# Eight-row and one-row matmuls widened to 128 rows, and two reorderings of VectorE's queue, in a Fourier and attention encoder

## The chip, the core and the metric

The kernel runs on one core of a Trainium2 chip. The metric is the device time of one execution, in microseconds (us), lower is better. Five engines run their own instruction queues side by side: TensorE (PE in the profile, its weight loads are PEld), VectorE (DVE), ScalarE (ACT), GpSimd (POOL) and SyncE (SP, which here only issues DMAs).

## What is computed

The reference runs two independent sequences of 512 tokens with 1024 features through two layers. Layer 0 mixes tokens by a 2-D Fourier transform, layer 1 by attention with 8 query heads and 2 key heads; each is followed by an MLP with a squared ReLU and 4096 hidden features:

```python
def fourier_mix(h, w_out):
    hg = h.reshape(B, S, 8, 128)                       # 8 groups of 128 features
    f = jnp.fft.fft2(hg, axes=(1, 3), norm="ortho").real
    return f.reshape(B, S, 1024) @ w_out

def sq_relu_mlp(h, w_up, w_down):
    a = jnp.maximum(h @ w_up, 0)
    return (a * a) @ w_down

x = x + fourier_mix(rms_norm(x), w_out);  x = x + sq_relu_mlp(rms_norm(x), ...)   # layer 0
x = x + gqa_attention(rms_norm(x), ...);  x = x + sq_relu_mlp(rms_norm(x), ...)   # layer 1
return rms_norm(x)
```

All arithmetic is float32. The kernel gets its precision out of float32r operands: each operand is split into a high and a low part, and a product is three matmuls (high by high, high by low, low by high). `split` (L80 to L82) does this: ScalarE casts the high part (L81), then VectorE, or in some places GpSimd, subtracts it from the source for the low part (L82).

## The kernel before, in words

**Shared tiles.** On-chip tiles come from pools with a fixed number of buffers: 38 of one size for activations and operands (`slot`), 8 half-size ones (`tm`), 5 for raw weights (`raw`), 4 for split weights (`w`), 8 PSUM banks (`ps`). A load waits until a buffer of its pool is free. The compiler's scheduler fixes each engine's order from the program's order and its own estimates; inside `tc.manual_schedule(engines=...)` the named engines keep the written order of the instructions of that block.

**The Fourier stage** (L273 to L690, all five engines in written order). The transform over the 512 tokens uses the symmetry of cosine and sine: `Front` normalizes the input, folds feature d with its mirror image and token s with token 512 - s, and leaves an even part `ee`, an odd part `oo` (two chunks c of 128 tokens each) and eight columns `ny`. `transform(q)` (L440) then works for sequence q:

- `seq_nyq` and `seq_part` (L399, L403) multiply by the cosine and sine tables: for each of four blocks j of 128 features, and each chunk c, three matmuls into `o` and three into `v`. With c = 1, `seq_even` adds the token in the middle, whose cosine is +1 or -1: two matmuls over one single row (L395, L396), row 0 of `oo` (or `ny`) against row 0 of the table `altT`.
- `seq_evac` (L411) splits `o` and `v` out of PSUM into operands `a` and `b`.
- `feat_stage` (L419) transforms over the features in a group: three matmuls on `a`, two over eight rows (L423, L424: `nyqT`, 8 rows, against `an`, the split of `seq_nyq`'s eight rows), three on `b`, two into `en` (L427, L428). Its results are split into `uv[q, j]`. `nyq_out` (L434) makes `un[q]` of `en`.
- `even_outs` and `odd_outs` (L535, L538) multiply `uv` by the output weights, which `Fold` has folded meanwhile: sums and differences of weight rows on GpSimd and VectorE (L479, L482), high parts on ScalarE (L486), low parts on VectorE (L490) or GpSimd (L82). `even_outs` needs `uv[q, 3]` for its last block k = 3, and at the end `un[q]` (L532).

For sequence 0 the results wait aside (`Aside.move`) and are added to the residual later: the even half on GpSimd (`ev.add`, L571 to L573), the odd half on VectorE (`od.add`, L568 and L569). `ev.add` runs during `transform(1)`, and `od.add(j)` stands in VectorE's queue inside `transform(1)`, ahead of the splits of `feat_stage(j)` (`between`, L454 to L464). Then follow `even_outs(1, ...)`, whose results VectorE adds (L543, L544), `odd_outs(1, ...)` (L548, L549), the sums of squares, and the normalized operands of the MLP (`Blocks`).

**The MLP** multiplies pairs of 128-row blocks in a 2-by-2 scheme with seven block products in place of eight: sums of operand blocks on the one side, sums of weight blocks on the other. `first_product` (L751) does 14 pairs p. `Pair.rest(p)` (L815) has five products, each 12 matmuls of 128x512: `ob`, `oc`, `od`, then `a22` on top of `oc`, then `s4` on top of `od`. After each product VectorE adds the result up: u2 (L819), u3 (L821), u3 again (L829), v (L838), t (L843). The fourth product needs L821 to have read `oc`, the fifth needs L829 to have read `od`. Between these stand the weight sums and splits of the next pair: `sums_23` (L796 to L798), `split_23`, `sum_4` (L802), `split_1`, `split_4` (all L82). For p < AHEAD = 6 VectorE keeps the written order; from p = 6 on, each pair has seven products in `rest`'s period and the scheduler orders VectorE. `Pair.out` then makes sums of the results on GpSimd (L851 to L854) and writes seven spill tensors, on ScalarE's and SP's queues.

The last pair, 13, has no next pair. After it, four `Regular` blocks r0 to r3 (L859) go through `w_up` without the scheme, and `second_product` begins, which reads the spilled operands back: `moving` (L948) loads an operand by DMA and splits it. The generator `ahead` (L1032) issues the first of these loads early; the operands of its first groups are b11, b21 (four pairs) and t2, t1, t3, b22, t4 (two pairs).

Of the kernel before, what the change touches and what calls it, by code (L numbers as in the profile page):

```python
# [18 lines left out]
P = 128  # L19
# [20 lines left out]
def trunk_kernel(ctx, tc, x_in, xt_in, y_out, dcos, dsin, feat, rope, gfour, gcol, grow, gfin,  # L40
# [19 lines left out]
    def slot(shape, dt):  # L60
        return act.tile(shape, dt, tag="u4", name=nm("u"))
# [235 lines left out]
    gr, rcos, rsin, rft, gc = begin()  # L297
    tabs = [slot([P, D], F32R) for _ in range(2)]
    cosT = [t[:, :516].rearrange("p (a b) -> p a b", a=2) for t in tabs]
    altT = tabs[0][0:1, 516:774]  # L300
    pickT = tabs[1][:, 516:594]
    sinT = slot([P, 2, 512], F32R)
    fslot = slot([P, D], F32R)
    ft = fslot[:, :512].rearrange("p (a b) -> p a b", a=2)
    nyqT = fslot[0:8, 512:1024]

    def table_cos():
        for c in range(2):
            split(cosT[c][:, 0], cosT[c][:, 1], rcos[:, c * 258 : (c + 1) * 258])
        nc.scalar.copy(altT, rcos[0:1, 516:774])  # L310

    def table_sin():
        split(sinT[:, 0], sinT[:, 1], rsin)

    def table_feat():
        split(ft[:, 0], ft[:, 1], rft[:, :256])
        nc.scalar.copy(nyqT, rft[0:8, 334:846])
        nc.scalar.copy(pickT, rft[:, 256:334])


# [77 lines left out]

    def seq_nyq(q, c, o):  # L399
        seq_even(o[0:8, :258], [ny[q, c][:, i, 0:8] for i in range(2)],  # L400
                 [ny[q, 0][0:1, i, 8:16] for i in range(2)], c)

    def seq_part(q, j, c, o, v):  # L403
        js = slice(j * P, (j + 1) * P)
        seq_even(o[:, :258], [ee[q, c][:, i, js] for i in range(2)],
                 [oo[q, 0][0:1, i, js] for i in range(2)], c)
        cs = slice(c * 256, (c + 1) * 256)
        mm3(v[:, :256], oo[q, c][:, 0, js], oo[q, c][:, 1, js],
            sinT[:, 0, cs], sinT[:, 1, cs], c == 0, c == 1)
# [9 lines left out]
    def feat_stage(q, j, a, b, an, en):  # L419
        u, v = ps(), ps()  # L420
        mm3(u[:, :258], ft[:, 0, 0:P], ft[:, 1, 0:P], a[:, 0], a[:, 1], True, False)
        nyt = nyqT[:, j * P : (j + 1) * P]
        nc.tensor.matmul(u[:, :258], nyt, an[0:8, 0], start=False, stop=False)  # L423
        nc.tensor.matmul(u[:, :258], nyt, an[0:8, 1], start=False, stop=True)  # L424
        mm3(v[:, :256], ft[:, 0, P:], ft[:, 1, P:], b[:, 0], b[:, 1], True, True)
        ent = pickT[:, 6 - 2 * j : 78 - 2 * j]
        nc.tensor.matmul(en[0:72, :258], ent, a[:, 0], start=j == 0, stop=False)  # L427
        nc.tensor.matmul(en[0:72, :258], ent, a[:, 1], start=False, stop=j == 3)  # L428
        t = slot([P, 2, 512], F32R)
        split(t[:, 0, 0:257], t[:, 1, 0:257], u[:, :257])  # L430
        split(t[:, 0, 257:], t[:, 1, 257:], v[:, 1:256])
        uv[q, j] = t

    def nyq_out(q, en):  # L434
# [2 lines left out]
        nc.vector.tensor_sub(t[64:72], en[64:72, :258], f32(t[64:72]))  # L437
        un[q] = t

    def transform(q, mid=lambda: None, between=lambda j: None):  # L440
        on, ov = ps(), [(ps(), ps()) for _ in range(3)]
        seq_nyq(q, 0, on)
        for j in range(3):
            seq_part(q, j, 0, *ov[j])
        mid()
        en = ps()
        seq_nyq(q, 1, on)
        an = slot([P, 2, 258], F32R)
        split(an[0:8, 0], an[0:8, 1], on[0:8, :258])
        ab = []  # L450
        for j in range(3):
            seq_part(q, j, 1, *ov[j])
            ab.append(seq_evac(*ov[j]))
        between(0)  # L454
        feat_stage(q, 0, *ab[0], an, en)
        o3 = ps(), ps()
        for c in range(2):
            seq_part(q, 3, c, *o3)
        between(1)
        feat_stage(q, 1, *ab[1], an, en)  # L460
        ab.append(seq_evac(*o3))
        between(2)
        feat_stage(q, 2, *ab[2], an, en)
        between(3)  # L464
        feat_stage(q, 3, *ab[3], an, en)
        nyq_out(q, en)
# [275 lines left out]
    def product(o, w, h, first=True):  # L742

        n = len(h)
        for k in range(n):
            sl = slice(k * P, (k + 1) * P)
            for i, (x, y) in enumerate(((0, 0), (0, 1), (1, 0))):
                nc.tensor.matmul(o, w[x][:, sl], h[k][y], start=first and k + i == 0,  # L748
                                 stop=k == n - 1 and i == 2, skip_group_check=not first)

    def first_product(l, blocks, rows, ahead):  # L751
        def b(name):
            return [(h[0][:, i], h[1][:, i]) for h in blocks.b[name] for i in range(2)]
# [10 lines left out]
        class Pair:  # L764
# [47 lines left out]
                self.s4 = h[:, 0], h[:, 1]  # L812
                split(*self.s4, self.x4)

            def rest(self, nxt):  # L815
                ob, oc, od = ps(), ps(), ps()
                u2, u3, t = tm(), tm(), self.t
                product(ob, self.s2, b("t2"))
                nc.vector.tensor_add(u2, ob, t[:, 0])  # L819
                product(oc, self.s3, b("t3"))  # L820
                nc.vector.tensor_add(u3, oc, u2)  # L821
                if self.p >= AHEAD:
                    self.second()
                if nxt:
                    nxt.sums_23()
                product(od, self.s1, b("t1"))
                if nxt and nxt.p >= AHEAD:
                    nxt.split_row()
                nc.vector.tensor_add(u3, od, u3)  # L829
                if nxt:  # L830
                    nxt.split_23()
                squares(u3, u3)
                product(oc, self.a22, b("t4"), False)
                if nxt:
                    nxt.sum_4()
                    nxt.split_1()
                v = tm()
                nc.vector.tensor_add(v, oc, u2)  # L838
                squares(v, v)
                if nxt:  # L840
                    nxt.split_4()
                product(od, self.s4, b("b22"), False)
                nc.vector.tensor_add(t[:, 0], od, u2)  # L843
                squares(t[:, 0], t[:, 0])
                return t[:, 1], t[:, 0], v, u3
# [72 lines left out]
        for p, pair in enumerate(pairs[:-1]):  # L918
# [9 lines left out]
                last[0].load()  # L928
            pair.out(*done)

        pairs[-1].first()
        with tc.manual_schedule(engines={ET.DVE}):
            done = pairs[-1].rest(None)
        with tc.manual_schedule(engines={ET.SP}):
            for r in last[1:]:
                next(ahead)
                r.load()
            for _ in ahead:
                pass
            pairs[-1].out(*done)  # L940
# [3 lines left out]
    def second_product(l, blocks, rows):  # L944
# [84 lines left out]
            for op in (("b11", "b21"), ("t2", "t1", "t3", "b22", "t4"))[i][slice(*ops)]:  # L1029
                b[op] = moving(op, g, n)  # L1030

        def ahead():  # L1032
            n = SUM_GROUPS[0][1]
            group(0, 0, ROW_GROUPS[0][1])
            yield
            group(1, 0, n, (0, 2))
            yield
            group(1, 0, n, (2, 5))
            yield
            early[0, 0, 0] = row_raw(0, 0, ROW_GROUPS[0][1])  # L1040
            for q in range(NSEQ):
                residual(q, 0)
            early[1, 0, 0] = sums_raw(0, 0, n)
            for q in range(NSEQ):
                residual(q, 1)

        first_product(l, blocks, rows, ahead())
        e += [tm() for _ in range(4)]
        for _, i, m, g, n in sorted(steps):
            if m == 0 and g > 0:  # L1050
# [498 lines left out]
```

## Time and profile before

| | us |
|---|---|
| three runs, median (lowest to highest) | 1784.64 (1781.79 to 1785.09) |
| the profiled execution | 1783.47 |
| its span, first to last instruction | 1781.7 |
| around the span (difference) | 1.77 |
| TensorE busy, share of the span | 1722.3, 97% |
| VectorE busy | 1225.2, 69% |
| mean granted TensorE clock | 0.982 |

The span is what the profile shows; the 1.77 us around it are taken to be unchanged. The profile's times are us from the start of the span. In a timeline a row has start, duration, engine, line, operation, output<-inputs, shape and count, and in brackets the engine's idle time before it and what ended it. In a table of windows, each row has the window, its length, and for each engine its busy time and (in brackets) the instructions begun, then the granted clock of TensorE as a share of full speed. In the table of waits a row has who waited for whom: total us, times, longest.

### The profile page before, as it was taken

Reading aid. Unit: us, or ns where it says so; the run is one execution under the profiler, and the core shown is the slowest. Engines: PE = TensorE matmul, PEld = TensorE weight load, DVE = VectorE, ACT = ScalarE, POOL = GpSimd, SP = SyncE. Lnnn points to the kernel's source line nnn. Section 1 sums busy time; section 2 is a strip of 40 time slices with the busy share of each in tenths; the row PEclk is TensorE's granted clock in tenths of the full one; section 3 lists DMA queues with packets and bytes.
Section 4 is the critical chain, followed back from the end, with each engine's and each line's share of the span. In section 5 each row is a group of like instructions: output and inputs, shape, how many; then the busy total and the mean of one; then the engine's idle time right before and its main releaser. Section 6 shows DMA issues by size and latency. Waiting matters only on the chain. (4 is left out here: it accounts for less than half of the span.)

```text
span 1781.7 us, 22113 instructions
## 1 busy us (share of the span) xinstructions
PE 1722.3 (97%) x7918; PEld 1417.7 (80%) x7918; DVE 1225.2 (69%) x1777; ACT 867.0 (49%) x1531; POOL 478.4 (27%) x382
## 2 busy tenths in 40 slices
PE   5999999999999999999999999999999999999997
PEld 4887877887778778878877888787788877878777
DVE  6867777455787686666578853687845478686765
ACT  4556545445534242345687733564544554343234
POOL 3550143223221111243334302204332232111103
PEclk7889999999999999999999999999999999999999
DMA  7234355337865353431100122224544486364232
GB/s 279 102 119 136 113 184 198 144 136 265 286 199 195 130 183 101 166 124 48 48 24 1 49 94 107 95 95 180 204 154 148 182 320 230 128 224 163 99 107 95
DMA packets 101670, 260.83 MB, mean 146 GB/s; under 512 B 10024, under 2 KB 10024, under 8 KB 101560
## 3 DMA queue, kind: packets, MB, share of 16 engines
q1 hardware_dynamic: 87160, 233.20, 37.4%
q10 hardware_dynamic: 14400, 26.22, 3.9%
q8 instruction: 62, 1.02, 0.2%
q14 instruction: 48, 0.39, 0.1%
HBM read 187.03 MB, written 72.35 MB: 146 GB/s over the span
## 5 line engine op out<-in xcount | busy, mean ns | idle before, releaser
L748 PE MATMUL ps<-u,w 128*128 128x512 f32 x4752 | 1094.6, 391 | 14.6 <-DVE u L960 8.0
L748 PEld LDWEIGHTS ps<-u,w 128*128 128x128 f32 x4752 | 889.0, 188 | 213.3 <-issue 9.3
L81 ACT CAST w<-raw 128x1024 fp32r<-128x1024 f32 (+2 forms) x250 | 232.0, 932 | 488.5 <-PE ps L748 299.4
L82 DVE TENSOR_TENSOR w<-raw,w 128x1024 fp32r<-128x1024 f32 (+2 forms) x246 | 274.1, 1117 | 65.7 <-ACT w L81 64.9
L82 DVE TENSOR_TENSOR u<-u,u 128x1024 fp32r<-128x1024 f32 x122 | 162.3, 1346 | 25.4 <-ACT u L81 25.2
L960 DVE TENSOR_TENSOR u<-ps,u 128x512 f32<-128x512 f32 x160 | 109.7, 687 | 97.8 <-PE ps L748 97.2
L81 ACT CAST u<-u 128x1024 fp32r<-128x1024 f32 x123 | 126.5, 1050 | 81.6 <-DMA u<-spill_b 61.9
L851 POOL TENSOR_TENSOR u<-u 128x512 f32<-128x512 f32 x28 | 38.3, 1367 | 446.2 <-ACT u L762 446.2
L1005 POOL TENSOR_TENSOR raw<-raw,raw 128x512 f32<-128x512 f32 (+1 forms) x32 | 43.4, 1356 | 419.0 <-DVE raw L1004 376.2
L76 PE MATMUL ps<-u,u 128*128 128x512 f32 (+2 forms) x392 | 153.2, 393 | 2.4 <-ACT u L561 1.6
L77 PE MATMUL ps<-u,u 128*128 128x512 f32 (+2 forms) x392 | 147.2, 376 | 1.5 <-DVE u L82 1.5
L78 PE MATMUL ps<-u,u 128*128 128x512 f32 (+2 forms) x392 | 147.2, 375 | 0.6 <-POOL u L82 0.6
L154 POOL TENSOR_TENSOR t<-t,t 128x512 f32<-128x512 f32 (+1 forms) x56 | 75.8, 1354 | 213.6 <-ACT t L152 153.8
L82 DVE TENSOR_TENSOR u<-ps,u 128x512 fp32r<-128x512 f32 (+4 forms) x126 | 76.6, 627 | 23.9 <-ACT u L81 22.8
L76 PE MATMUL ps<-u,w 128*128 128x512 f32 (+2 forms) x256 | 91.4, 357 | 0.9 <-ACT w L81 0.9
L732 DVE TENSOR_TENSOR u<-ps,u 128x512 f32<-128x512 f32 (+1 forms) x64 | 41.9, 656 | 72.7 <-PE ps L78 72.7
L78 PE MATMUL ps<-u,w 128*128 128x512 f32 (+2 forms) x256 | 90.8, 356 | 0.5 <-DVE w L82 0.5
L77 PE MATMUL ps<-u,w 128*128 128x512 f32 (+2 forms) x256 | 90.8, 355 | 0.0
L76 PEld LDWEIGHTS ps<-u,u 128*128 128x128 f32 x392 | 78.7, 201 | 15.1 <-ACT u L81 2.5
L77 PEld LDWEIGHTS ps<-u,u 128*128 128x128 f32 x392 | 79.1, 202 | 13.1 <-DVE u L82 4.2
L748 PE MATMUL ps<-u,u 128*128 128x512 f32 x336 | 82.0, 393 | 7.6 <-DVE t L829 7.6
L78 PEld LDWEIGHTS ps<-u,u 128*128 128x128 f32 x392 | 78.6, 201 | 12.8 <-POOL u L82 0.8
(210 smaller groups left out, 2141.9 us busy)
## 6 DMA issues: line engine op xcount, KB each, us to landing
raw<-w_up SPq DMA_DIRECT2D x84, 512.0 KB, 4.0
u<-spill_t SPq DMA_DIRECT2D x56, 512.0 KB, 6.6
raw<-w_sum SPq DMA_DIRECT2D x48, 512.0 KB, 3.6
spill_t<-u SPq DMA_DIRECT2D x84, 256.0 KB, 2.0
u<-spill_b SPq DMA_DIRECT2D x42, 512.0 KB, 5.8
spill_b<-t ACTq DMA_DIRECT2D x56, 256.0 KB, 2.0
park<-u SPq DMA_DIRECT2D x24, 512.0 KB, 2.6
raw<-w_row SPq DMA_DIRECT2D x24, 512.0 KB, 3.4
```

The lines of the kernel that those rows point to most:

```text
L76: nc.tensor.matmul(out, lh, rh, start=first, stop=False)
L77: nc.tensor.matmul(out, lh, rl, start=False, stop=False)
L78: nc.tensor.matmul(out, ll, rh, start=False, stop=last)
L81: nc.scalar.copy(dst_hi, src)
L82: eng.tensor_sub(dst_lo, src, f32(dst_hi))
L154: nc.gpsimd.tensor_add(acc[q][:, :n], acc[q][:, :n], s[:, :n])
L732: nc.vector.tensor_add(x[:, :n], o[:, :n], x[:, :n])
L748: nc.tensor.matmul(o, w[x][:, sl], h[k][y], start=first and k + i == 0, stop=k == n - 1 and i == 2, skip_group_check=not first)
L851: nc.gpsimd.tensor_sub(t[:, 0], b12, b11)
L960: nc.vector.tensor_add(x, o, x)
L1005: nc.gpsimd.tensor_sub(a11, a11, a21)
```

## The change

It has three parts.

1. **128 rows.** `altT` and `nyqT` become tables with all 128 partitions (the rows beyond the first one, or the first eight, are zero in the input tables), and the matmuls at L395, L396, L423 and L424 take all 128 rows of `oo`, `ny` and `an`. `an` is allocated once ahead of both transforms, and GpSimd sets it to zero at the start of the kernel.
2. **`rest` of every pair but the last.** `sums_23` of the next pair moves ahead of the product `oc` and its sum L821 (for p = 0 it stays behind L821), and `split_23` moves from behind L829 to ahead of the product `od`, so ahead of L829; `split_row` (p >= 5) comes behind it.
3. **The last pair.** VectorE and SP keep the written order there, and `ahead` is stepped from inside `rest`: b11's load and split and r1's load ahead of the product `od` and L829; b21's and r2's load ahead of L838; t2's, t1's and r3's load ahead of the last product and L843. The rest of `ahead` follows after it.

```diff
-    altT = tabs[0][0:1, 516:774]
+    altT = tabs[0][:, 516:774]
-    nyqT = fslot[0:8, 512:1024]
+    nyqT = fslot[:, 512:1024]
...
-        nc.scalar.copy(altT, rcos[0:1, 516:774])
+        nc.scalar.copy(altT, rcos[:, 516:774])
-        nc.scalar.copy(nyqT, rft[0:8, 334:846])
+        nc.scalar.copy(nyqT, rft[:, 334:846])
...
-                 [ny[q, 0][0:1, i, 8:16] for i in range(2)], c)
+                 [ny[q, 0][:, i, 8:16] for i in range(2)], c)
-                 [oo[q, 0][0:1, i, js] for i in range(2)], c)
+                 [oo[q, 0][:, i, js] for i in range(2)], c)
...
-        nc.tensor.matmul(u[:, :258], nyt, an[0:8, 0], start=False, stop=False)
-        nc.tensor.matmul(u[:, :258], nyt, an[0:8, 1], start=False, stop=True)
+        nc.tensor.matmul(u[:, :258], nyt, an[:, 0], start=False, stop=False)
+        nc.tensor.matmul(u[:, :258], nyt, an[:, 1], start=False, stop=True)
...
+    an = slot([P, 2, 258], F32R)
+    nc.gpsimd.memset(f32(an), 0.0)
     def transform(q, mid=lambda: None, between=lambda j: None):
-        an = slot([P, 2, 258], F32R)
...
-            def rest(self, nxt):
+            def rest(self, nxt, fill=iter(())):
                 product(ob, self.s2, b("t2"))
                 nc.vector.tensor_add(u2, ob, t[:, 0])
+                if nxt and self.p > 0:
+                    nxt.sums_23()
                 product(oc, self.s3, b("t3"))
                 nc.vector.tensor_add(u3, oc, u2)
                 if self.p >= AHEAD:
                     self.second()
                 if nxt:
-                    nxt.sums_23()
-                product(od, self.s1, b("t1"))
+                    if self.p == 0:
+                        nxt.sums_23()
+                    nxt.split_23()
                 if nxt and nxt.p >= AHEAD:
                     nxt.split_row()
+                next(fill, None)
+                product(od, self.s1, b("t1"))
                 nc.vector.tensor_add(u3, od, u3)
-                if nxt:
-                    nxt.split_23()
                 squares(u3, u3)
                 product(oc, self.a22, b("t4"), False)
                 if nxt:
                     nxt.sum_4()
                     nxt.split_1()
+                next(fill, None)
                 v = tm()
                 nc.vector.tensor_add(v, oc, u2)
                 squares(v, v)
+                next(fill, None)
                 if nxt:
                     nxt.split_4()
                 product(od, self.s4, b("b22"), False)
...
+        ahead = ahead(last[1:])
         pairs[-1].first()
-        with tc.manual_schedule(engines={ET.DVE}):
-            done = pairs[-1].rest(None)
+        with tc.manual_schedule(engines={ET.DVE, ET.SP}):
+            done = pairs[-1].rest(None, ahead)
         with tc.manual_schedule(engines={ET.SP}):
-            for r in last[1:]:
-                next(ahead)
-                r.load()
             for _ in ahead:
                 pass
...
-        def ahead():
+        def ahead(regular):
             n = SUM_GROUPS[0][1]
-            group(0, 0, ROW_GROUPS[0][1])
+            group(0, 0, ROW_GROUPS[0][1], (0, 1))
+            regular[0].load()
+            yield
+            group(0, 0, ROW_GROUPS[0][1], (1, 2))
+            regular[1].load()
             yield
             group(1, 0, n, (0, 2))
+            regular[2].load()
             yield
             group(1, 0, n, (2, 5))
-            yield
             early[0, 0, 0] = row_raw(0, 0, ROW_GROUPS[0][1])
```

More of the change, by code (lines that the diff above doesn't have):

```diff
@@ L1045, in ahead @@
                 residual(q, 1)
-        first_product(l, blocks, rows, ahead())
+        first_product(l, blocks, rows, ahead)
         e += [tm() for _ in range(4)]
```

## The prediction

> **What bounds the kernel now.** First the page, then the waits of TensorE.
>
> ```profile
> span 1781.7 us, 22113 instructions
> ...
> PEclk7889999999999999999999999999999999999999
> ```
> ```profile
> PE ps L748 <- DVE t L829: 7.6, 10, 1.7
> ```
>
> TensorE is the busiest engine throughout, so time can come only from its clock or its waits. Two entries touch the change: the clock of the first three slices (45 us each), and 7.6 us of waits for L829 in ten places. Next, four windows of the Fourier stage (two from transform(0), two round transform(1)), and single matmuls.
>
> ```profile
> 28.86:32.27 3.41, 3.41 (x13) 2.50 (x12) 1.53 (x4) 1.30 (x4) 3.41 (x2) 0.50 0.88 348
> 49.34:52.75 3.41, 3.41 (x17) 3.41 (x17) 3.28 (x7) 0.72 (x3) 3.41 (x2) 0.50 0.01 2
> 76.65:80.06 3.41, 1.83 (x14) 1.22 (x13) 2.84 (x7) 2.40 (x6) 0.00 (x0) 1.00 0.07 26
> 100.54:103.95 3.41, 3.41 (x17) 3.21 (x16) 1.81 (x4) 2.43 (x6) 0.00 (x0) 0.50 0.80 262
> ```
> ```profile
> 28.85 0.42 PE L78 MATMUL ps<-u,u 128*128 128x256 f32 x1
> 29.20 0.58 PE L395 MATMUL ps<-u,u 1*128 1x258 f32 x1
> ...
> 30.30 0.42 PE L77 MATMUL ps<-u,u 128*128 128x258 f32 x1
> 30.52 0.42 PE L78 MATMUL ps<-u,u 128*128 128x258 f32 x1
> ```
> ```profile
> 53.04 0.28 PE L78 MATMUL ps<-u,w 128*128 128x258 f32 x1
> 53.16 0.28 PE L76 MATMUL ps<-u,w 128*128 128x258 f32 x1
> ```
>
> At half clock matmuls start 0.215 us apart (30.30 to 30.52), at full clock 0.12 (53.04 to 53.16). Round a narrow pair the five steps from 28.85 to 30.52 take 1.67 us in place of 5 x 0.215 = 1.07, so 0.6 are lost. A window with narrow pairs (28.86) begins 13 matmuls at clock 0.50. The first one without any (49.34) begins 17, and behind it the steps are 0.12: the clock is up. Transform(1) does the same up to 103.95. It had lost its clock behind 76.65 to 80.06, where TensorE had work for 1.83 of 3.41 us. So the narrow pairs hold the clock down, by their gaps or by their few rows. The Trainium skill (TensorE: Matmul & The Clock Gate, "What's actually happening") has the clock decided in free-running windows of 3413 ns; the trace agrees, both releases lie 15 of them apart (103.95 - 52.75 = 51.20). The sum does without it.
>
> **Part 1, transform(0).** TensorE's half clock hardly matters here:
>
> ```profile
> 35.34 3.50 DVE L490 TENSOR_TENSOR w<-u,w 128x1024 fp32r<-128x1024 f32 x1 [0.52 <-ACT w L486]
> ```
> ```profile
> 35.39 2.36 POOL L479 TENSOR_TENSOR u<-raw,u 128x1024 f32<-128x1024 f32 x1
> ```
> ```profile
> 65.94 0.39 PE L78 MATMUL ps<-u,u 128*128 128x256 f32 x1 [0.56 <-POOL u L82]
> ```
>
> Without gaps the c = 1 parts (24 matmuls x 0.215) end 1.7 us earlier, so L490 may start at 33.6. But it takes 3.50 us beside GpSimd's fold, and the two mostly take turns, so an earlier start lengthens GpSimd's op. At 65.94 TensorE waits for GpSimd's last odd weight already, however early it comes there. I take 0.3 us gained, between 0 and 1.7.
>
> **Part 1, transform(1).** From 80 us on VectorE and GpSimd again share work: `ev.add` fills GpSimd, and `od.add(j)` waits for `ev.add(j)`.
>
> ```profile
> 82.16 1.26 POOL L571 TENSOR_TENSOR u<-u,u 128x512 f32<-128x512 f32 x1
> ...
> 93.81 0.63 POOL L573 TENSOR_TENSOR u<-u,s 128x2 f32<-128x2 f32 x1
> ```
> ```profile
> L569 DVE TENSOR_TENSOR u<-u,u x4: 683/1218/1757, 89.1 to 100.4; 128x510 f32<-128x510 f32 x4
> ```
> ```profile
> 102.68 0.42 DVE L437 TENSOR_TENSOR u<-ps,u 8x258 fp32r<-8x258 f32 x1
> ```
> ```profile
> 108.65 0.64 PE L532 MATMUL ps<-u,u 72*128 72x258 f32 x4
> ```
>
> L569 takes 1.76 us beside GpSimd and 0.68 alone. At full clock the c = 1 part of block 0 is held to 82.2 by the low part of `oo`, GpSimd's op before 82.16; 17 more matmuls x 0.12 bring block 2 to 84.3, and VectorE has split it at 85.0. Then it does, in order: `od.add(0)` beside GpSimd, two ops of 1.75: 88.5; two splits out of PSUM (0.35 each): 89.2; `od.add(1)`, likewise 3.3: 92.5; four splits: 93.9; `od.add(2)`, mostly beside `ev.add(3)`: 96.2; two splits, `od.add(3)` alone (0.68 twice, less overlap), two splits: 98.9. L437 starts there, 3.8 us ahead of 102.68. TensorE meanwhile can do k = 0 to 2 of `even_outs`, 36 matmuls; 9 of them early, 27 once a fourth PSUM bank is read, with `feat_stage(2)`'s first split at 96.6. At full clock they end at 99.9 and the last 16 (12 for k = 3, 4 for L532) at 101.8, against 108.65 + 0.64 = 109.3 now: 7.5 us gained. At half clock they end at 105.8: 3.5 gained. TensorE also waits for block 3's operands, from 90.4 (ten matmuls behind the splits at 89.2) to 93.9, and the row of 76.65 says that such a wait costs the clock for a while: a window of 3.41 us at half clock begins 16 matmuls in place of 28, so 12 x 0.12 = 1.5 us, 6.0 gained. I take 5.8. From 109 us the sums of squares, L118 to L132 and the MLP's first operands hang on these results on all engines, so the lead is kept.
>
> GpSimd's zeroing of `an` lies ahead of its first work at 27 us and ScalarE copies as many columns as before; if something else waited there, it would be by an op of some 0.6 us (half of L571's 1.26).
>
> **Part 2.** What `rest(3)` of layer 0 does now:
>
> ```profile
> 233.85 0.69 DVE L819 TENSOR_TENSOR t<-ps,u 128x512 f32<-128x512 f32 x1 [0.63 <-issue]
> 236.57 0.69 DVE L821 TENSOR_TENSOR t<-ps,t 128x512 f32<-128x512 f32 x1 [2.03 <-PE ps L748]
> 237.17 1.16 DVE L796 TENSOR_TENSOR raw<-raw,raw 128x512 f32<-128x512 f32 x1
> 238.37 1.66 DVE L797 TENSOR_TENSOR raw<-raw 128x512 f32<-128x512 f32 x1
> 240.07 1.66 DVE L798 TENSOR_TENSOR raw<-raw,raw 128x512 f32<-128x512 f32 x1
> 241.65 0.68 DVE L829 TENSOR_TENSOR t<-ps,t 128x512 f32<-128x512 f32 x1
> 242.90 1.22 DVE L82 TENSOR_TENSOR w<-raw,w 128x1024 fp32r<-128x1024 f32 x1 [0.57 <-ACT w L81]
> ```
> ```profile
> 242.48 0.70 PE L748 MATMUL ps<-u,u 128*128 128x512 f32 x2 [0.57 <-DVE t L829]
> ```
>
> TensorE resumes 0.83 us after L829 starts, 0.73 late. That is the wait the edit removes. In its place the sums stand ahead of L821: they start when L819 ends (234.45) and take 4.48 as here (241.65 - 237.17). Elsewhere they take less: alone 3 x 0.68, in `rest(5)` 0.72 + 2 x 1.66 = 4.04:
>
> ```profile
> L797 DVE TENSOR_TENSOR raw<-raw x28: 683/692/1667, 162.1 to 1377.3; 128x512 f32<-128x512 f32 x28
> ```
> ```profile
> 266.07 0.72 DVE L796 TENSOR_TENSOR raw<-raw,raw 128x512 f32<-128x512 f32 x1
> ```
> ```profile
> 198.09 0.68 DVE L829 TENSOR_TENSOR t<-ps,t 128x512 f32<-128x512 f32 x1
> ```
>
> L821 then starts at 238.93, and the fourth product, which needs it, resumes at 239.76; it is due when `od` ends, at 236.57 - 0.28 + 2.73 = 239.02 (a product is 12 starts of 0.2275). So TensorE waits 0.74 there, as much as before; with 4.04, 0.30. Ahead of L829 the split now queues: ScalarE's cast, VectorE's subtraction (242.90 - 241.73 = 1.17 behind the sums' end, then 1.13), so L829 at about L821 + 2.4, in time for the fifth product, for which it may start up to L821 + 2.73. Per layer: `rest(2)` to `rest(4)` unchanged (4.48); `rest(1)`, without a wait now, +0.7; `rest(0)`, where the split moves L829 from 198.09 (the third row) by 2.3 to 200.4 against 200.0 that would do (L821 would start at 195.4, two products later less 0.83), +0.4; `rest(5)`, where `split_row` (1.13) stands ahead of L829 before and after, +0.1. Sum +1.2, both layers +2.4 us. With 4.04: -0.9 a layer, -1.9. With the sums wholly interleaved with GpSimd (three ops of 1.7, 5.1): +4.5 for both. The weights they read are loaded a pair ahead. The Trainium skill (SBUF — State Buffer, "Who interferes with whom") calls the port that VectorE and GpSimd share an exclusive lock; L796 to L798 beside GpSimd fit it, and it speaks against this edit, which moves the sums to where GpSimd's `out` may run.
>
> **Part 3.** L829 already stands behind b11's two splits in the last pair, so that wait (1.7 us at longest) stays.
>
> ```profile
> 419.87 2.47 SPq L953 DMA_DIRECT2D u<-spill_t  x2
> 424.70 0.35 SPq L90 DMA_DIRECT2D raw<-w_up  x1
> ```
> ```profile
> 430.33 0.68 DVE L843 TENSOR_TENSOR u<-ps,t 128x512 f32<-128x512 f32 x1
> 430.93 1.22 DVE L82 TENSOR_TENSOR w<-raw,w 128x1024 fp32r<-128x1024 f32 x1
> ```
>
> t2's and t1's loads move behind r2's, from 419.87 to 425.1, and their splits ahead of L843, which comes some 4 us later. Only ScalarE's squares and GpSimd's `out` wait for L843. r1's split (430.93) is due at 435; if it stays behind L843, TensorE waits 1.2 us a layer; if the scheduler lets it pass, nothing. I take 0, with 2.4 as the other end.
>
> **Sum.** -0.3 - 5.8 + 2.4 + 0 = -3.7: a profiled execution of 1783.47 becomes 1779.8. The median of the runs is 1.2 above that execution; I forecast 1780.5, between.
>
> **Rivals.** (a) *More:* the sums fit (4.04, or less) and the clock holds: -0.3 - 7.5 - 1.9, so 1774. For it: the 4.04 of `rest(5)`. Against it: VectorE and TensorE wait on each other in transform(1). (b) *The clock stays low:* transform(1) is bound by VectorE, GpSimd and gaps even with 128 rows: part 1 gives 0.6, the sum is +1.8, 1786. The Trainium skill ("Why this matters for your kernels", same TensorE page) has a single 32-row matmul last as long as a 128-row one, by which widening would gain nothing; the 0.6 us round each pair contradict it. (c) *Slower:* the sums on VectorE, ahead of L821, meet GpSimd's `out` in full (5.1, a wait of 1.36), and `split_23` meets its tail and doubles (+0.5): 1.9 us for `rest(1)` to `rest(4)`, 2.8 for `rest(5)`, 0.4 for `rest(0)`, 10.8 a layer against half of 7.6 now: +14.0, less 6.1: 1792. For it: GpSimd starts early if L843 does. It decides from about 1.2 us a pair. (d) *r1's split behind L843:* +2.4, 1783.
>
> **Chances.** Forecast 0.45 (own range 1777 to 1783), (a) 0.17, (b) 0.13, (c) 0.13, (d) 0.12. A change of 0.2%, 3.6 us, is about what a measurement can tell from none. Faster: 0.35 of the forecast's 0.45 and all of (a), 0.52. Slower: 0.10 of (c) and 0.03 of (b), 0.13. Same: 0.35. Range 1773 to 1788: it leaves out the far parts of (a) and (c).
>
> **What would show it.** The profile after: L395 and L423 with 128 rows and no gaps; granted clock 1.00 between 82 and 94 us; L437 near 98.5, L532 ending near 103. In `rest(1)` to `rest(4)`: TensorE waiting for L821 in place of L829, 0.3 to 0.8 us each. L843 of pair 13 behind two more splits. Wrong it would be if transform(1) keeps half clock, if waits for L829 remain beside those for L821, or if new waits stand between 425 and 450 us.

## The result, and the profile after

| | before | after |
|---|---|---|
| median beside each other (5 runs each) | 1782.78 us | 1774.47 us (1772.22 to 1777.02) |
| ratio, 95% interval | | 0.9951 (0.9937 to 0.9966) |
| the same kernels measured again (11 and 5 runs) | 1783.74 us | 1772.23 us, ratio 0.9939 (0.9926 to 0.9952) |
| profiled execution, its span | 1783.47, 1781.7 us | 1774.45, 1772.7 us |

The change is worth about 9 us, 0.5%, where 4 were forecast; the time lies inside the stated range of 1773 to 1788, outside the forecast's own 1777 to 1783, and at the rival "more" (1774). To see where it came from, take VectorE instructions that both kernels have and measure from one to the next (us; the last column is the kernel after, profiled a second time). The stages add up to the spans.

```
stage                                              before    after    after, again
start to the first L819 (rest(0), layer 0)         192.57   186.50   183.82
rest(0) to rest(5), layer 0                         88.26    87.59    87.59
rest(6) to rest(12)                                133.17   133.28   133.28
last pair, L819 to L829                             11.59    10.23     9.84
from there to the second product's first add        31.00    30.99    31.01
second product                                     271.85   270.95   272.70
to rest(0) of layer 1                              459.25   459.15   457.88
rest(0) to rest(5), layer 1                         88.44    87.77    87.72
rest(6) to rest(12)                                132.96   133.28   133.28
last pair, L819 to L829                             10.46    10.79    10.76
from there to the second product's first add        31.04    30.99    30.99
second product                                     272.81   272.87   271.43
to the end                                          58.27    58.26    58.28
```

So the first stage gives 6 to 9 us, `rest(0)` to `rest(5)` 0.7 in each layer (the seven pairs behind them give 0.1 to 0.3 back), and what the last pair and the second product show changes sign between layers and executions. Line numbers have moved: L819, L821, L829, L838, L843 are now L821, L825, L836, L844, L850; the sums L796 to L798 are L798 to L800; `od.add` (L568, L569) is L570, L571; GpSimd's `out` is L858 to L861; L532 is L534. L395, L423 and L437 kept theirs.

**Transform(1).** First a timeline of TensorE in the kernel after, then its windows (the stretches that the prediction showed of before, and the later ones).

```profile
82.18 0.39 PE L78 MATMUL ps<-u,u 128*128 128x256 f32 x1 [0.67 <-POOL u L82]
82.41 0.28 PE L395 MATMUL ps<-u,u 128*128 128x258 f32 x1
82.52 0.28 PE L396 MATMUL ps<-u,u 128*128 128x258 f32 x1
82.64 0.28 PE L76 MATMUL ps<-u,u 128*128 128x258 f32 x1
```
```profile
83.47:86.89 3.42, 3.42 (x31) 3.42 (x30) 3.10 (x6) 1.92 (x6) 3.42 (x4) 1.00 0.00 0
86.89:90.30 3.41, 2.97 (x25) 2.76 (x24) 3.41 (x5) 1.93 (x6) 3.41 (x4) 1.00 0.34 141
90.30:93.71 3.41, 0.87 (x4) 0.87 (x5) 3.41 (x6) 0.00 (x0) 3.41 (x4) 0.77 0.34 141
93.71:97.12 3.41, 3.41 (x18) 3.41 (x18) 3.41 (x6) 2.64 (x6) 1.19 (x2) 0.50 0.30 121
```

The one-row pairs, now with 128 rows, start 0.11 to 0.12 apart like their neighbours: the gaps are gone. In the window from 83.47 TensorE begins 31 matmuls; before it began 13 to 17 in every window from 80.06 to 103.95. From 90.30 on VectorE and GpSimd are busy without a break (3.41 each) and TensorE has work for 0.87 us: the bound has moved to the two engines that share `od.add` and `ev.add`, and the wait costs the clock (half speed from 92.15 to 98.98, so the two last rows have 0.77 and 0.50). The stage still ends earlier:

```profile
98.01 0.42 DVE L437 TENSOR_TENSOR u<-ps,u 8x258 fp32r<-8x258 f32 x1
```
```profile
102.37 0.28 PE L78 MATMUL ps<-u,w 128*128 128x258 f32 x1
102.49 0.64 PE L534 MATMUL ps<-u,u 72*128 72x258 f32 x4
102.97 0.28 PE L76 MATMUL ps<-u,w 128*128 128x258 f32 x1
```

L437 starts at 98.0; it was forecast near 98.5 and stood at 102.7 before. L534 ends at 103.1; that was forecast near 103 and stood at 109.3 before.

**rest(3) and rest(1).** VectorE in `rest(3)` of layer 0, then GpSimd beside it:

```profile
228.70 0.69 DVE L821 TENSOR_TENSOR t<-ps,u 128x512 f32<-128x512 f32 x1 [2.08 <-PE ps L750]
229.31 0.68 DVE L798 TENSOR_TENSOR raw<-raw,raw 128x512 f32<-128x512 f32 x1
230.03 1.67 DVE L799 TENSOR_TENSOR raw<-raw 128x512 f32<-128x512 f32 x1
231.73 1.66 DVE L800 TENSOR_TENSOR raw<-raw,raw 128x512 f32<-128x512 f32 x1
233.31 0.68 DVE L825 TENSOR_TENSOR t<-ps,t 128x512 f32<-128x512 f32 x1
```
```profile
228.02 1.29 POOL L858 TENSOR_TENSOR u<-u 128x512 f32<-128x512 f32 x1 [7.37 <-ACT u L764]
229.39 1.75 POOL L859 TENSOR_TENSOR u<-t,u 128x512 f32<-128x512 f32 x1
```

The three sums take 4.00 us here (229.31 to 233.31), not 4.48: the first takes 0.68, for it starts in the gap between two of GpSimd's operations. In `rest(1)` GpSimd begins later, while L821 runs, and all three sums interleave, 5.06 us (200.47 to 205.53):

```profile
200.47 1.74 DVE L798 TENSOR_TENSOR raw<-raw,raw 128x512 f32<-128x512 f32 x1
202.24 1.67 DVE L799 TENSOR_TENSOR raw<-raw 128x512 f32<-128x512 f32 x1
203.94 1.66 DVE L800 TENSOR_TENSOR raw<-raw,raw 128x512 f32<-128x512 f32 x1
205.53 0.68 DVE L825 TENSOR_TENSOR t<-ps,t 128x512 f32<-128x512 f32 x1
```
```profile
200.38 1.28 POOL L858 TENSOR_TENSOR u<-u 128x512 f32<-128x512 f32 x1 [69.86 <-ACT u L764]
```

The waits of TensorE over the whole kernel, where before had 7.6 us in ten places for L829:

```profile
PE ps L750 <- DVE t L836: 2.4, 4, 0.9
...
PE ps L750 <- DVE t L825: 1.9, 2, 1.0
```

The two for L825 are `rest(1)` of both layers; in the four for L836 are `rest(5)` and the last pair of both. This table counts from the modelled end of the matmul before. Waits given below are counted from when the next matmul was due, which adds 0.16 us: 1.15 in `rest(1)`, 0.77 in `rest(5)`.

### The profile page after: what moved, and what is told of

The parts are those of the page before. It is cut to its first block, busy times and chain, and to the rows that moved or that the text cites. A ratio compares the mean times of both kernels' runs of the same rounds, so it can differ in the third digit from the quotient of the medians.

```text
span 1772.7 us, 22129 instructions
## 1 busy us (share of the span) xinstructions
PE 1703.8 (96%) x7918; PEld 1403.0 (79%) x7918; DVE 1226.3 (69%) x1777; ACT 868.2 (49%) x1531; POOL 487.9 (28%) x383
## 5 line engine op out<-in xcount | busy, mean ns | idle before, releaser
L858 POOL TENSOR_TENSOR u<-u 128x512 f32<-128x512 f32 x28 | 37.2, 1328 | 450.8 <-ACT u L764 450.8
L77 PE MATMUL ps<-u,u 128*128 128x512 f32 (+2 forms) x392 | 144.8, 369 | 10.8 <-DVE u L82 10.6
L76 PE MATMUL ps<-u,u 128*128 128x512 f32 (+2 forms) x392 | 148.9, 382 | 2.8 <-ACT u L563 1.5
L78 PE MATMUL ps<-u,u 128*128 128x512 f32 (+2 forms) x392 | 144.7, 369 | 2.2 <-POOL u L82 2.2
L77 PEld LDWEIGHTS ps<-u,u 128*128 128x128 f32 x392 | 75.9, 194 | 22.8 <-DVE u L82 13.9
L78 PEld LDWEIGHTS ps<-u,u 128*128 128x128 f32 x392 | 75.5, 193 | 14.8 <-POOL u L82 2.9
L76 PEld LDWEIGHTS ps<-u,u 128*128 128x128 f32 x392 | 75.7, 193 | 13.8 <-ACT u L81 2.1
```

The costliest lines, as they stand in the source:

```text
L76: nc.tensor.matmul(out, lh, rh, start=first, stop=False)
L77: nc.tensor.matmul(out, lh, rl, start=False, stop=False)
L78: nc.tensor.matmul(out, ll, rh, start=False, stop=last)
L858: nc.gpsimd.tensor_sub(t[:, 0], b12, b11)
```

## Each part alone

Theory A, formed from these two profiles: each part acts in its own place, and they add up to about 6, 1 and 0 us.

**Part 1 alone** (`e1_rows`): the slices of `altT`, `nyqT`, `an`, `ny` and `oo` widened and `an` zeroed as in the change, all else as before.

> Part 1 alone: 128 rows for both narrow pairs, all else as before. Theory A (each part acts in its own place, the parts add up): transform(1) gains 6.1 us as in the changed kernel, transform(0) nothing, so about 6.1 us faster than before; L437 of transform(1) at 98 in place of 102.7, granted clock 1.00 from 80 to 90 us. Rival B (the release of the clock at 80 us was a matter of where the clock's windows fell, not of the rows): with another offset of the windows the wait at 76.65 costs the clock again and the gain lies anywhere between 0 and 6 us. In both, rest(2) to rest(5) keep their waits for L829 (0.56, 0.73, 0.73 and 1.42 in the first layer).

1774.3 us, ratio 0.9951 (0.9939 to 0.9963): as much as the whole change. L437 comes at 97.9, L534's counterpart ends at 103.1, clock 1.00 from 80 to 92 us; the ten waits for the third row's add stay, 6.8 us in all. A stands, though its 6.1 is too small: the interval is 6.6 to 10.9 us.

**Part 2 alone** (`e2_sums`): only this in `rest`.

```diff
                 nc.vector.tensor_add(u2, ob, t[:, 0])
+                if nxt and self.p > 0:
+                    nxt.sums_23()
                 product(oc, self.s3, b("t3"))
...
                 if nxt:
-                    nxt.sums_23()
-                product(od, self.s1, b("t1"))
+                    if self.p == 0:
+                        nxt.sums_23()
+                    nxt.split_23()
                 if nxt and nxt.p >= AHEAD:
                     nxt.split_row()
+                product(od, self.s1, b("t1"))
                 nc.vector.tensor_add(u3, od, u3)
-                if nxt:
-                    nxt.split_23()
```

> Part 2 alone: new order of the weight sums and their splits, all else as before. Theory A: 0.6 us gained in the first layer and 0.35 in the second, as the changed kernel's rows have it: about 0.9 us faster than before, with waits for the third row's add in rest(1) (about 1.2 us, new) and small ones (0.24) in rest(2) to rest(4). The prediction's own term would be 2.4 us slower. Rival C: rest(1)'s wait is an accident of the first product's phase, not of the order; then it is absent here and about 3.3 us are gained.

1782.09 us, ratio 0.9999 (0.999 to 1.0007). `rest(0)` to `rest(5)` take 87.59 and 87.72 us, as in the changed kernel: 0.7 less a layer, and the 7 pairs behind them 0.1 to 0.3 more. `rest(1)` has its wait of 1.15 here too, so rival C falls. About 1 us is what the stages show; the medians can't separate it from nothing, but they exclude the 2.4 us slower of the prediction's term.

**Part 3 alone** (`e3_last`): `ahead` as a function of the regular blocks, its steps taken inside the last pair's `rest`, DVE and SP in written order, as in the change.

> Part 3 alone: order of the last pair, all else as before. Theory A: the order written out does not itself speed TensorE; the last pair's wait follows the landing of b11's load, which scatters by a microsecond from layer to layer; 0 +- 1.2 us. Rival D: with t2's, t1's and the weights' loads issued later, b11's load has the DMA engines to itself and its first cast comes 1.3 us earlier behind L819 than before in both layers (6.6 in place of 7.9): 1.5 to 2.5 us faster.

1784.17 us, ratio 1.0006 (0.9998 to 1.0015). The last pair's L819 to L829 takes 10.54 and 10.33 us. Over all kernels of this study, seven with the old last pair have 10.1 to 11.6 in layer 0 (mean 10.76) and 10.3 to 11.8 in layer 1 (10.77); seven with the new one 9.8 to 10.6 (10.37) and 10.3 to 11.4 (10.76). At most 0.4 us in one layer: rival D falls. In all 28 of these last pairs L829 or its counterpart starts 3.6 to 3.7 us behind the first cast of b11, which waits for the load; so the 1.4 us that the two profiles differ by in layer 0 is scatter in the landing of b11's load.

**Parts 1 and 2** (`e4_rows_sums`): both edits above together.

> Parts 1 and 2 without part 3. Theory A: 7.0 us faster than before (6.1 and 0.9), 1 to 2 us behind the changed kernel at most, and within noise of it if part 3 is worth nothing. Rival D: the same 7.0, and the changed kernel 1.5 to 2.5 us ahead of it by part 3.

1774.8 us, ratio 0.9954 (0.9942 to 0.9965), within noise of the changed kernel and of part 1 alone. Its first stage ends at 183.57, 3 us ahead of the two other profiles with part 1, though nothing of that stage differs. Its windows:

```profile
86.89:90.30 3.41, 1.37 (x12) 1.16 (x10) 3.41 (x5) 1.42 (x5) 3.41 (x4) 1.00 0.38 154
90.30:93.71 3.41, 2.49 (x11) 2.49 (x12) 3.41 (x6) 0.85 (x3) 2.98 (x3) 0.64 0.38 154
93.71:97.12 3.41, 3.41 (x27) 3.41 (x26) 3.07 (x8) 3.41 (x7) 1.32 (x2) 0.86 0.54 223
```

Transform(1) ran 1.5 us earlier (L437 of transform(0) at 50.6 in place of 52.1 and 52.2, with the clock up at 29.8 in place of 30.6 and 30.7), and the wait for VectorE cost one window at half clock (91.3 to 94.7) where the changed kernel paid two (92.1 to 99.0). Where the windows fall differs from execution to execution. With the narrow pairs the first stage took 192.57, 193.97 and 192.38 us; with part 1 it took 186.45, 183.57, 186.50, 183.82 and, in an experiment below, 185.13. The means differ by 7.9 us. That is the fair figure for part 1 in this stage, from three profiles and five; the 6.1 of the first pair of profiles is one draw.

## Gaps or rows

The prediction left open whether a narrow pair hurts by the gap round it or by its few rows. `e5_k64` gives both pairs 64 rows; `e9_alt` and `e10_nyq` widen one kind of pair to 128.

```diff
-    altT = tabs[0][0:1, 516:774]
+    altT = tabs[0][0:64, 516:774]
...
-    nyqT = fslot[0:8, 512:1024]
+    nyqT = fslot[0:64, 512:1024]
...
-        nc.tensor.matmul(u[:, :258], nyt, an[0:8, 0], start=False, stop=False)
+        nc.tensor.matmul(u[:, :258], nyt, an[0:64, 0], start=False, stop=False)
```

> Both narrow pairs get 64 rows in place of 1 and 8 (the rows added are zero), all else as before. Theory G (the loss comes from changing the number of rows from one matmul to the next: the weight load is then not hidden): the 0.6 us round each pair stay, L437 of transform(1) stays near 102.7 and the time near before, gain 0 to 1 us. Rival R (few rows cost by themselves, by the clock or in the array, in proportion to the rows): half of the gap and most of part 1's gain are there, 5 us or more faster than before.

1775.29 us, ratio 0.9965 (0.9951 to 0.9978), 6 us faster: G is wrong on the time. But the gap is where it was. A timeline of TensorE in `e5_k64` at half clock, then one at full clock:

```profile
28.87 0.41 PE L78 MATMUL ps<-u,u 128*128 128x256 f32 x1
29.22 0.58 PE L395 MATMUL ps<-u,u 64*128 64x258 f32 x1
29.60 0.42 PE L396 MATMUL ps<-u,u 64*128 64x258 f32 x1
29.95 0.58 PE L76 MATMUL ps<-u,u 128*128 128x258 f32 x1
30.33 0.42 PE L77 MATMUL ps<-u,u 128*128 128x258 f32 x1
```
```profile
90.33 0.28 PE L78 MATMUL ps<-u,u 128*128 128x258 f32 x1
90.55 0.39 PE L423 MATMUL ps<-u,u 64*128 64x258 f32 x1
90.77 0.28 PE L424 MATMUL ps<-u,u 64*128 64x258 f32 x1
90.98 0.39 PE L76 MATMUL ps<-t,u 128*128 128x256 f32 x1
91.21 0.28 PE L77 MATMUL ps<-t,u 128*128 128x256 f32 x1
```

28.87 to 30.33 is 1.46 us in place of 4 x 0.215 = 0.86: 0.6 lost with 64 rows, as with one. At full clock it is 0.88 in place of 0.48: 0.4 lost. So the gap hangs on the change of rows: it is the same for 64, 8 and 1. A change to 72 rows has none: the four of L534 above start 0.12 behind their neighbour at 102.37 and take 0.48 up to the next at 102.97. The Trainium skill (TensorEngine Tiling (Array Packing), "Key Properties", with the modes under "Available Configurations") has TensorE drain when its tiling mode changes, and lists modes of 128, 64 and 32 rows. The steps agree with that (a gap at 64, 8 and 1 rows, none at 72); that these matmuls ran in such modes is not shown.

R is right that the clock counts the rows: with the same gaps, but 64 rows, half clock ends at 38.7 us in transform(0) (52.8 before) and in transform(1) it lasts from 83.0 to 86.5 and from 96.7 to 100.1 (80.2 to 104.0 before). L437 comes at 99.4. Windows of half clock with one narrow pair each show it directly: first one of before (a one-row pair), then one of `e9_alt` below (an eight-row pair), then one of `e5_k64`.

```profile
35.78:39.19 3.41, 3.41 (x15) 2.96 (x15) 3.41 (x3) 1.32 (x2) 3.41 (x2) 0.50 0.45 154
```
```profile
44.89:48.30 3.41, 3.41 (x15) 3.06 (x15) 3.08 (x3) 2.94 (x4) 0.43 (x1) 0.50 0.39 157
```
```profile
83.05:86.46 3.41, 3.41 (x15) 2.96 (x15) 1.15 (x4) 1.13 (x3) 3.41 (x5) 0.50 0.02 5
```

TensorE is busy throughout and begins 15 matmuls in each. Behind the first two the clock stays at half; behind the third it is up. The rows are not all: in the second profile of the changed kernel, where every row of these pairs is used, half clock lasts from 40.4 to 54.1 while TensorE waits for VectorE in between. So both effects, gaps and rows, are there. By the ratios 64 rows bring 6.2 of the 8.7 us of part 1; the intervals overlap, so what the gaps cost by themselves is not separated from nothing.

**The one-row pairs alone** (`e9_alt`: only `altT`, `ny` and `oo` widened).

> Only the one-row pairs (L395, L396) get 128 rows, the eight-row pairs stay. Theory A: VectorE's chain of od.add and splits in transform(1) starts earlier by these pairs alone, the eight-row pairs then cost 0.3 to 0.6 us each behind it: 4 to 6 us faster than before, L437 near 98 and the end of L532 1 to 2 us behind that of the kernel with both. Rival H (one narrow pair in a window is enough to hold the clock at half): no more than 2 us.

1776.47 us, ratio 0.9969 (0.9958 to 0.998). L437 at 98.0, L532 ends at 103.7, 0.6 behind the kernel with both. Theory A; rival H falls by the time. The eight-row pairs don't bring the clock down: TensorE runs at full clock from 31 us on with eight-row pairs at 32.3, 35.6 and 37.2, until it runs out of work near 39. But one such pair held a window at half clock, the one from 44.89 above; in that, H is right.

**The eight-row pairs alone** (`e10_nyq`: only `nyqT` and `an`).

> Only the eight-row pairs (L423, L424) get 128 rows, the one-row pairs stay. Theory A: VectorE's chain in transform(1) is as late as before up to the last block, so 1 to 2.5 us faster than before. Rival: the eight-row pairs carry the gain (they stand in the later half, where TensorE is the bound): 5 us or more.

1777.6 us, ratio 0.9975 (0.9965 to 0.9985): 4.5 us faster, more than the 1 to 2.5 expected, less than the rival's 5. The one-row pairs hold half clock from 81.0, but it ends at 91.2 in place of 104.0. L437 comes at 99.4 and L532 ends at 103.0. This profile is of the fastest of the eight runs (1774.22 us), so its places flatter the edit. By the ratios the two kinds give 5.5 and 4.5 us, 10.0 in sum, against 8.7 for both together (6.6 to 10.9): whether they add up can't be told.

## Where the new order of the sums pays

`e8_from2` is the changed kernel with the new order from `rest(2)` on.

```diff
-                if nxt and self.p > 0:
+                if nxt and self.p > 1:
                     nxt.sums_23()
...
-                    if self.p == 0:
+                    if self.p < 2:
                         nxt.sums_23()
-                    nxt.split_23()
+                    else:
+                        nxt.split_23()
...
                 nc.vector.tensor_add(u3, od, u3)
+                if nxt and self.p < 2:
+                    nxt.split_23()
```

> The changed kernel, with the new order of sums and splits only from rest(2) on; rest(0) and rest(1) in the old order. Theory F (the first pair in the new order pays: its predecessor's last add is early, so GpSimd's out begins behind the first sum and all three sums interleave, 5.1 us): the wait of 1.16 us leaves rest(1) and appears in rest(2), 0.2 to 0.3 us a layer gained at most against the changed kernel. Rival P (it is the place of rest(1)): no wait above 0.3 in rest(1) to rest(4), 1.2 us a layer gained, 2.4 us faster than the changed kernel.

1774.71 us, ratio 0.9964 (0.9952 to 0.9976), not to be told from the changed kernel. The stage itself is measured well: 87.13 and 87.33 us against 87.59 and 87.77, so 0.45 a layer, where F had 0.2 to 0.3 at most. `rest(1)` has no wait, `rest(2)` has one of 0.72. F has the place right and the mechanism only in part: in `rest(2)` the first sum runs alone (0.68), and it is the split behind them that meets the tail of GpSimd's `out` and takes 2.31 in place of 1.23:

```profile
217.91 1.29 POOL L864 TENSOR_TENSOR t<-t,u 128x512 f32<-128x512 f32 x1
```
```profile
217.97 2.31 DVE L82 TENSOR_TENSOR w<-raw,w 128x1024 fp32r<-128x1024 f32 x1 [0.57 <-ACT w L81]
```

## The new bound: od.add on VectorE

In the changed kernel TensorE waits for the splits of block 3, which stand behind `od.add(1)`. (The 6.3 us in the first expectation below are transform(0)'s longest wait; the one at 91 us lasts 3.0.)

```diff
-        transform(1, between=lambda j: od.add(j, nc.vector))
+        transform(1, between=lambda j: j and od.add(j - 1, nc.vector))
+        od.add(3, nc.vector)
```

> The changed kernel, with each od.add(j) of transform(1) one place later on VectorE (behind one feature stage more), so that the splits of block 3 out of PSUM come ahead of od.add(1). Theory V (VectorE's order bounds transform(1) now: TensorE waits 6.3 us for those splits at 91 us, and the wait brings the clock down until 99): the wait shrinks below 4 us, L532 ends 1.5 to 3 us earlier than 103.1, and the time is 1.5 to 3 us below the changed kernel's. Rival W (the adds are needed by what follows): L437, the squares on ScalarE and GpSimd's L154 start later instead (95.5 and 97.4 now), the waits of TensorE near 122 and 134 grow by as much, and the time is that of the changed kernel or above it.

1772.15 us, ratio 0.9943 (0.9924 to 0.9962). The windows of `e11_add1`:

```profile
90.30:93.71 3.41, 3.10 (x26) 2.89 (x25) 3.41 (x6) 1.54 (x4) 3.41 (x4) 1.00 0.33 137
93.71:97.12 3.41, 3.35 (x28) 3.15 (x27) 3.35 (x5) 2.41 (x5) 2.65 (x3) 1.00 0.39 161
```

The wait is gone, the clock stays up, L534's counterpart ends at 98.0 and `rest(0)` begins at 181.52, 2.3 and 5.0 us earlier than in the two profiles of the changed kernel. V holds for the stage. On the time it is not shown: this ratio can't be told from the changed kernel's 0.9951 and 0.9939. 1.3 us are given back in `rest(0)` to `rest(5)` of layer 0 (88.87): in `rest(3)` L821's counterpart comes 0.4 us later behind the pair before it, all three sums interleave with GpSimd (4.87 us), and TensorE waits 1.38 us. All three kernels with moved adds have a wait of this kind there, with any start of the stage; its cause stays open.

`e12_add2` goes further:

```diff
-        transform(1, between=lambda j: od.add(j, nc.vector))
+        transform(1, between=lambda j: j > 1 and [od.add(i, nc.vector) for i in (2 * j - 4, 2 * j - 3)])
```

> The changed kernel, with od.add(0) and od.add(1) behind the splits of block 3, and od.add(2) and od.add(3) ahead of the last feature stage. Theory V: no wait of TensorE above 1 us before 95 us and no half clock there; L532 ends 2 to 5 us earlier than 103.1; 2 to 5 us below the changed kernel. Rival W: GpSimd's L154 waits for od.add and starts later than 97.4; same time as the changed kernel or slower.

1778.51 us, ratio 0.9976 (0.9965 to 0.9987): slower than `e11_add1` beside it, while the interval just touches that of the changed kernel (0.9966). Here `od.add(2)` and `od.add(3)` stand ahead of the last feature stage's splits, three of their four operations at 1.76 us beside GpSimd, and L437 comes at 101.5 (95.9 in `e11_add1`): the queue is made longer just ahead of what TensorE waits for, 2.8 us up to 94.9 and 1.5 up to 101.5. `rest(0)` begins at 186.89. V's rule was too simple: "later" alone does not help; what is ahead of a split that TensorE waits for counts.

Last, `e11_add1`'s and `e8_from2`'s edits together, with the changed kernel beside it on the same chip:

> The changed kernel with both improvements: od.add(j) of transform(1) one place later, and the new order of sums and splits from rest(2) on only. If the two savings seen so far (about 2 us and 0.9 us) are real and add up, 2 to 4 us below the changed kernel run beside it, L532's end near 98 and no wait of TensorE above 0.3 us in rest(1); if the first was chance of where the clock's windows fell, within 1 us of it.

> The changed kernel once more, beside the one above and on the same chip. Its time against before should repeat the ratio of 0.995; its profile gives another offset of the clock's windows: L532's end anywhere between 100.3 and 104, the waits of rest(1) (1.16 us) and rest(5) (0.77 us) as in its first profile, and the last pair's wait of 0.3 to 1.8 us as the landing of b11's load has it.

1771.3 us, ratio 0.993 (0.9916 to 0.9943), against 1772.23 us, ratio 0.9939 (0.9926 to 0.9952). The first stage and layer 1's rests save what they did alone (`rest(0)` at 181.34 against 183.82; 87.34 against 87.72), while `rest(0)` to `rest(5)` of layer 0 give 0.9 back (88.52 against 87.59). The medians differ by 0.9 us, within the 1 us expected if nothing was gained, and the intervals overlap by most of their length. It is the fastest median here and beats before; whether it beats the changed kernel stays open. The second profile of the changed kernel repeats the waits of `rest(1)` and `rest(5)`; L534 ends at 100.5, with one window at half clock (91.6 to 95.0).

## Why the prediction was right, and where it was not

**The bound and the place: right.** Time came from TensorE's clock and waits, and almost all of it from part 1.

**Part 1, transform(0): right.** 0.3 us were taken, between 0 and 1.7. L437 of transform(0) stands at 52.2 before and after; where the clock came up a window's part earlier, it stands at 50.6 and 50.7 (`e4_rows_sums`, `e14_after`), 1.5 us earlier. TensorE then waits for VectorE, 6.3 us at longest.

**Part 1, transform(1): right in mechanism, small in size.** The working by VectorE's queue put L437 at 98.9 and the end at 101.8 plus 1.5 for one window at half clock; the first profile has 98.0 and 103.1. That the end fits is partly luck: VectorE came 0.9 us sooner than worked out, and TensorE paid two windows, not one. The other profiles with part 1 show one or two, and the mean over all of them is 7.9 us for the whole first stage against the 6.1 forecast: that term was too small. Of the signs given, the clock of 1.00 up to 94 us did not come (0.77 in the window from 90.30). Rival (b), a clock that stays low, falls with `e1_rows`. The sentence "by their gaps or by their few rows" is settled so far: the rows hold the clock with the gaps unchanged, and how much the gaps add stays open. The Trainium skill's 32-row rule (TensorE: Matmul & The Clock Gate, "Why this matters for your kernels") holds for the matmul alone: the second of a pair takes 0.28 us at full clock with 8, 64 and 128 rows, only the first, behind the change of rows, 0.38 to 0.39 with 8 and 64. What widening saves is the change of rows and the clock.

**Part 2: wrong in sign; the step that failed is the 4.48.** `rest(3)`'s sums were measured where they stood, behind L821, and moved with their duration. But it is their overlap with GpSimd that makes it, and that moved too: 4.00 in `rest(2)` to `rest(4)`. The same working with 4.04, the prediction's other end, gave -1.9 us; the stages show about -1. In detail (layer 0, from L819 to the next L819): `rest(2)` to `rest(4)` were to stay and lose 0.39, 0.56 and 0.55 us; `rest(1)` was to cost 0.7 and costs 1.28; `rest(0)` was to cost 0.4 and costs 0.03; `rest(5)` was to cost 0.1 and gains 0.48. Rival (c), all sums interleaved at 5.1, is what `rest(1)` alone does in the changed kernel, at 5.06; TensorE's wait there, 1.15, is above the 0.3 to 0.8 that were to show it. And waits for L829's counterpart remain beside those for L825, in `rest(5)`, which the prediction named as a sign of being wrong.

**Part 3: right at 0.** Rival (d)'s wait is absent: from L829 to the second product's first add it is 31.00 and 30.99 us. r1's split now stands ahead of L844, and GpSimd's `out` of the last pair starts 4.4 us later behind its L819 (23.7 in place of 19.2), and the stretch to the second product's first add is no longer for it.

**The sum.** -3.7 was forecast, about -9 measured: of the difference part 2 is 3.4 (-1.0 for +2.4), part 1 is 1.8 (-7.9 for -6.1). The rest is within the intervals.

## What to carry to other kernels

A matmul with 64, 8 or 1 rows among full ones cost more than its own time here: look at the starts of its neighbours, and at the clock of its window. Padding with zeros cost next to nothing: a matmul takes no longer, and GpSimd's zeroing of `an` took 0.53 us at 1.25 us, long before its first work at 27. When an operation on VectorE is moved, don't move its duration with it: the sums, which read SBUF twice, took 0.68 or 1.67 us, so ask what GpSimd does in the new place. A stage whose clock is decided in windows of 3.4 us scatters with where they fall (183.6 to 186.5 us here); average several profiles before a microsecond is put down to an edit.

## What was not expected of the hardware

The granted clock of the records starts late in some executions. A window of the kernel after, and its matmuls in that window:

```profile
28.86:32.27 3.41, 3.41 (x22) 3.41 (x23) 1.79 (x5) 1.82 (x6) 3.41 (x2) 1.00 0.84 330
```
```profile
29.03 0.42 PE L395 MATMUL ps<-u,u 128*128 128x258 f32 x1
29.24 0.42 PE L396 MATMUL ps<-u,u 128*128 128x258 f32 x1
29.46 0.42 PE L76 MATMUL ps<-u,u 128*128 128x258 f32 x1
```

The clock is given as 1.00, and the matmuls start 0.21 apart, the step of half clock; single weight loads take 0.28 to 0.34 us until 30.7 and 0.19 behind it. So the mean clock of a run can mislead: of 23 runs of before, 14 have a mean clock of 0.983 or 0.984 and a mean time of 1782.91 us, 9 have 0.990 to 0.992 and 1782.75 us. (Half clock from 25.5 to 52.9, if the records lack it, is 0.008 of the mean; that this is what those 9 lack is argued, not shown.) The Trainium skill (TensorE: Matmul & The Clock Gate, "Seeing it yourself") warns that these records were seen to be unreliable; the trace agrees. The step between matmuls is the better clock.
